# A two-layer encoder trunk on one Trainium2 core: high weight halves placed 192 bytes into wider tiles in the feature-major panels, with three small edits around it

## The chip, the core and the metric

The kernel runs on one core of one Trainium2 chip. The metric is the device time of one execution in microseconds (us); lower is better.

## The reference

The reference is two layers over an input `x` of 256 tokens by 2,048 features in float32, and a final RMSNorm. Each layer is a token mixer and a gated feed-forward network, each behind an RMSNorm and added to the residual stream:

```python
for layer in range(DEPTH):                      # DEPTH = 2
    h = _rmsnorm(x, norm_mix_g[layer])
    x = x + (_mixer_ab(...) if layer % 2 == 0 else _mixer_cd(...))
    h = _rmsnorm(x, norm_ffn_g[layer])
    x = x + _conv_ffn(h, ffn_w_up[layer], ...)  # (silu(g) * a) @ w_down, D_FF = 5632
return _rmsnorm(x, final_norm_g)
```

`_mixer_ab` projects to 7,168 columns, runs 8 heads of stick-breaking attention and 4 heads of differential attention, and projects back. `_mixer_cd` does the same with 4 heads of retention and a spatial-gating MLP. `_conv_ffn` projects to 2 x 5,632 columns, applies a causal depthwise convolution of width 3, gates, and projects back. Nearly all arithmetic is in the weight matrices, some 410 MB of float32, each read once.

## The kernel before

**Precision by splitting.** Each float32 weight block is split into a high half `hi` (a rounded copy in the type fp32r, written by ScalarE) and a low half `lo = raw - hi` (VectorE). The activations are split in the same way. TensorE then multiplies halves and adds the products up in PSUM.

**Loading.** `load_split` (L239) is the one place where weights come in. It takes a `raw` tile (128 partitions x 2,048 float32, three buffers, 1 MB), fills it by DMAs on the SyncE queue (SP) in `pieces` parts, and makes two `hi` and two `lo` tiles of 128 x 1,024 (five buffers each, L254 and L255). A tile of 1,024 float32 takes 4,096 bytes in each partition.

**Two ways to multiply.** `fm_panel` (L265) makes feature-major output for the query and key projections and for the up-projections of both feed-forward networks. One panel is 512 output features over 16 blocks of 128 input features, in four `load_split` calls. Here the weights are the stationary operand: for each of four groups of 128 output features (`m`) and four input blocks (`k`) there are two matmuls, called a pair below:

```python
nc.tensor.matmul(banks[m], hi[k][:, m * P:(m + 1) * P], xr, ...)                  # L272, 512 columns stream
nc.tensor.matmul(banks[m][:, :T], lo[k][:, m * P:(m + 1) * P], xr[:, :T], ...)    # L275, 256 columns stream
```

`xr` is an activation tile of 128 x 512 (its 256 high columns, then its 256 low ones). So `hi` meets both halves of the activation, `lo` the high half alone. Each matmul loads its own 128 x 128 stationary block before it streams. `tm_chunk` (L295) makes token-major output for all other projections. There the activation is stationary and the weights stream, in triples (L291 to L293): 512 columns each, 256 in the last quarter of `final` (L331).

**Addresses.** The pools lie one behind another in each partition: `raw`, `hi`, `lo`, the activations (`act`, 2,048 bytes a tile), then the small pools. Every `hi`, `lo` and activation tile is a multiple of 512 bytes long, and a stationary block of 128 float32 columns is 512 bytes. So before the change every block that a split matmul loads and every activation that it streams begins at the same place within 512 bytes.

**Order of the work.** Tasks (`start`, `pump`, `until`) put the small work of heads and norms between matmuls. The tile framework sets the order on each engine and the waits, from the program's order, the buffers and its own estimate of times. The first projection (`vb0`, L467) is built by hand with its activations: `First.load` sends the transposed input `x_t` on the ScalarE queue, `first_x` splits it between the weight casts, and the norm weights `gcols` (L451) scale it. 13 `warm` matmuls (L456) run on TensorE while the first data is on its way. In front of the second mixer the bias `sgu_b` comes in as a tile `sbr` (L660) and is transposed on TensorE into `sb_p` (L664).

Of the kernel before, what the change touches and what calls it, by code (L numbers as in the profile page):

```python
# [9 lines left out]
F32 = mybir.dt.float32  # L10
BF16 = mybir.dt.bfloat16
F32R = mybir.dt.float32r
# [6 lines left out]
P = 128  # L19
# [8 lines left out]
NEG = -3.0e38  # L28
ORDERED = {mybir.EngineType.DVE, mybir.EngineType.Activation}
GROUPS = (8, 12, 12, 12)  # L30


@with_exitstack
def trunk_kernel(
# [26 lines left out]
    nc = tc.nc  # L61
    cp = ctx.enter_context(tc.tile_pool(name="cp", bufs=1))
    wp = ctx.enter_context(tc.tile_pool(name="wp", bufs=3))
# [5 lines left out]
    def acc(name):  # L69
        return pp.tile([P, 512], F32, tag="acc", name=name, bufs=6)  # L70

    def small(name):
        return pp.tile([P, 512], F32, tag="small", name=name, bufs=2)
# [7 lines left out]
    def w15(name, n=384, dt=F32):  # L81
        return kp.tile([P, n], dt, tag="w15", name=name, bufs=10)
# [25 lines left out]
    def pump():  # L108
        for task in list(tasks):
            task[1] -= 1  # L110
            if task[1] <= 0:
                step(task)
# [123 lines left out]

    cnt = [0]

    def load_split(src, k, pieces=1, size=1024, before=None):  # L239
        cnt[0] += 1  # L240
        i = cnt[0]
        f = src.shape[-1]
        raw = wp.tile([P, 2048], F32, tag="raw", name=f"raw{i}")
        m = k * f
        rv = raw[:, :m].rearrange("p (k f) -> p k f", k=k)
        sv = src.rearrange("(k p) f -> p k f", p=P)
        kp_ = k // pieces
        for j in range(pieces):
            nc.sync.dma_start(rv[:, j * kp_:(j + 1) * kp_, :], sv[:, j * kp_:(j + 1) * kp_, :])
        his, los = [], []  # L250
        for j in range(0, m, 1024):
            if before is not None:
                before(j // f)
            hi = wp.tile([P, 1024], F32R, tag="hi", name=f"hi{i}_{j}", bufs=5)  # L254
            lo = wp.tile([P, 1024], F32R, tag="lo", name=f"lo{i}_{j}", bufs=5)  # L255
            for b in range(0, 1024, size):
                nc.scalar.copy(hi[:, b:b + size], raw[:, j + b:j + b + size])  # L257
                nc.vector.tensor_tensor(  # L258
                    lo[:, b:b + size], raw[:, j + b:j + b + size], hi[:, b:b + size].bitcast(F32), ALU.subtract)
            for b in range(0, 1024, f):  # L260
                his.append(hi[:, b:b + f])
                los.append(lo[:, b:b + f])
        return his, los

    def fm_panel(w, c0, xs, name):  # L265
        banks = [acc(f"fm_{name}{m}") for m in range(4)]
        for k0 in range(0, KT, 4):
            hi, lo = load_split(w[k0 * P:(k0 + 4) * P, c0:c0 + 512], 4)
            for m in range(4):
                for k in range(4):  # L270
                    xr = xs[k0 + k].rearrange("p a t -> p (a t)")
                    nc.tensor.matmul(  # L272
                        banks[m], hi[k][:, m * P:(m + 1) * P], xr,
                        start=(k0 + k == 0), stop=False, skip_group_check=True)
                    nc.tensor.matmul(  # L275
                        banks[m][:, :T], lo[k][:, m * P:(m + 1) * P], xr[:, :T],
                        start=False, stop=(k0 + k == KT - 1), skip_group_check=True)
                if m % 2 == 1:
                    pump()
        return banks  # L280
# [7 lines left out]
    def tm_mm(bank, a, t, hi, lo, st, sp):  # L288
        xh = a[:, 0, t * P:(t + 1) * P]
        xl = a[:, 1, t * P:(t + 1) * P]  # L290
        nc.tensor.matmul(bank, xh, hi, start=st, stop=False)  # L291
        nc.tensor.matmul(bank, xh, lo, start=False, stop=False)  # L292
        nc.tensor.matmul(bank, xl, hi, start=False, stop=sp)  # L293

    def tm_chunk(w, parts, n0, name, hook=None):  # L295
        banks = [acc(f"tm_{name}{t}") for t in range(2)]
        total = sum(nk for _, _, nk in parts)
        seen = 0
        for r0, xs, nk in parts:
            for k0 in range(0, nk, 4):  # L300
                kn = min(4, nk - k0)
                src = w[r0 + k0 * P:r0 + (k0 + kn) * P, n0:n0 + 512]
                if hook is None:
                    hi, lo = load_split(src, kn)
                else:
                    first = k0 == 0
                    with tc.manual_schedule(engines=ORDERED) if first else nullcontext():
                        hi, lo = load_split(
                            src, kn, 4 if first else 2, 512 if first else 1024, hook(k0))
                for k in range(kn):  # L310
                    st, sp = seen == 0, seen == total - 1
                    seen += 1
                    a = xs[k0 + k]
                    for t in range(2):
                        tm_mm(banks[t], a, t, hi[k], lo[k], st, sp)
                    if k % 2 == 1:
                        pump()
        return banks

    def residual(w, parts, norm, name):  # L320
        for n in range(4):
            banks = tm_chunk(w, parts, n * 512, f"{name}{n}")
            for t in range(2):
                xc = x_sb[:, t, n * 512:(n + 1) * 512]
                nc.vector.tensor_tensor(xc, banks[t], xc, ALU.add)
                if norm is not None:
                    norm.square(n, t)
            if norm is not None:
                start(norm.task(n), 1)
# [53 lines left out]
    def ffn(layer, norm, nxt, cols):  # L383
# [3 lines left out]
        def panel(kt0, which):  # L387
            return fm_panel(up, which * DFF + kt0 * P, norm, f"u{which}{layer}_{kt0}")
# [31 lines left out]
        early = None  # L420
        for gi, gs in enumerate(GROUPS):
            hs = []
            last = gi == len(GROUPS) - 1
            for kt0 in range(f0, f0 + gs, 4):
# [24 lines left out]
        return res  # L449

    gcols = cp.tile([P, 4, KT], F32, name="gcols")  # L451
    nc.gpsimd.dma_start(gcols, gains)
    gmix0, gffn0, gmix1, gffn1 = (gcols[:, i, :] for i in range(4))
    warm = small("warm")
    for i in range(13):
        nc.tensor.matmul(warm[:, :P], ones, ones, start=True, stop=True)  # L456
    n0 = First(gmix0, "n0")
    nc.scalar.activation(n0.rstd[:, :1], zeros, AF.Copy)
# [5 lines left out]
    def first_x(k0):  # L464
        return lambda i: n0.split(xts[k0 // 4], k0 // 4, i)

    vb0 = tm_chunk(w_in, ((0, n0, KT),), 5120, "vb0", first_x)  # L467
    def tm_copy(banks, rstd, name):
        v = m4(f"v_{name}")
# [11 lines left out]

    start(first_v(), 1)
    qb0 = fm_panel(w_in, 3072, n0, "qb0")
    until(lambda: vs)

# [41 lines left out]
    def fm_heads(c0, row, name, banks=None):  # L527
        banks = banks or fm_panel(w_in, c0, n0, name)
        dst = m4(f"qk_{name}").rearrange("p (m t) -> p m t", m=4)
        for m in range(4):  # L530
            fm_sum(banks[m], dst[:, m, :], row, f"{name}{m}")
        return dst
# [88 lines left out]
    for c in range(2):  # L621
        v = vs[0] if c == 0 else tm_copy(tm_chunk(w_in, ((0, n0, KT),), 5632, "vb1"), n0.rstd, "vb1")
        q = fm_heads(3072 + c * 512, n0.row, f"qb{c}", qb0 if c == 0 else None)
        k = fm_heads(4096 + c * 512, n0.row, f"kb{c}")
        for hh in range(2):
            start(diff_head(c * 2 + hh, q[:, hh * 2:hh * 2 + 2, :], k[:, hh * 2:hh * 2 + 2, :],
                            v, hh * 256), 2 + 2 * hh)
    for c in range(2):
        v = tm_copy(tm_chunk(w_in, ((0, n0, KT),), 2048 + c * 512, f"va{c}"), n0.rstd, f"va{c}")
        q = fm_heads(c * 512, rowq, f"qa{c}")  # L630
        k = fm_heads(1024 + c * 512, n0.row, f"ka{c}")
# [25 lines left out]
    for g in range(4):  # L657
        nc.tensor.transpose(ps[:, g * P:(g + 1) * P], sw[:, g, :], ident)
    nc.vector.tensor_copy(swt.rearrange("p g i -> p (g i)"), ps)
    sbr = cp.tile([4, P], F32, name="sbr")  # L660
    nc.sync.dma_start(sbr, sgu_b[0])
    sb = cp.tile([P, 4], F32, name="sb")
    ps = small("sb_p")
# [235 lines left out]
```

## Time and profile before

| | us |
|---|---|
| median of 3 runs | 2210.32 |
| runs | 2210.32, 2658.7, 2210.18 |
| profiled execution, own time | 2209.91 |
| its span, first to last instruction | 2208.2 |
| TensorE matmul busy (share of span) | 2195.7 (99%) |
| TensorE weight loads busy | 1868.6 (85%) |
| VectorE busy | 1414.1 (64%) |
| ScalarE busy | 1131.7 (51%) |
| GpSimd busy | 341.8 (15%) |

The profiled execution is a single one. Its own time is 1.7 us over its span and within 0.5 us of the median. A matmul's bar in the profile reaches from its first column to its modelled end, and the bars of neighbours overlap. So the pace of TensorE is read from the distance between starts, and not from the length of the bars.

### The profile page before, as it was taken

To read this page: it belongs to the slowest core of one execution; us is meant where nothing else is said; L and a number is where in the kernel's file an instruction comes from. 1 tells how busy PE (TensorE), PEld (TensorE's weight loads), DVE (VectorE), ACT (ScalarE), POOL (GpSimd) and SP (SyncE) were. 2 spreads that over 40 slices of the span, in tenths; PEclk is the share of its full clock that TensorE was granted. 3 is DMA by queue.
4 is the path that set the end of the run, shared out by engine and by line. 5 is a ranking of instruction groups with operands and counts; after the bars stand their busy time and mean duration, and the time that the engine had idled before them with its cause. 6 is when DMAs were issued, how large, how long until landed. Compare 5 with 4: busy or idle time off the path is not lost.

```text
span 2208.2 us, 29090 instructions
## 1 busy us (share of the span) xinstructions
PE 2195.7 (99%) x11297; PEld 1868.6 (85%) x11297; DVE 1414.1 (64%) x1796; ACT 1131.7 (51%) x1658; POOL 341.8 (15%) x538
## 2 busy tenths in 40 slices
PE   9999999999999999999999999999999999999998
PEld 8888888888888888888888888888888888888886
DVE  5655555586666577567756545567757757665775
ACT  6544545464554455355554455445545545544553
POOL 0110120031221022022103000002212102210320
PEclk9999999999999999999999999999999999999999
DMA  9555455556556555655655556555655655555553
GB/s 322 200 173 192 160 196 178 181 182 210 174 189 201 180 191 183 198 172 193 201 182 176 187 174 202 178 180 191 201 172 191 200 181 191 190 192 189 173 187 137
DMA packets 209903, 416.78 MB, mean 189 GB/s; under 512 B 6957, under 2 KB 10325, under 8 KB 209765
## 3 DMA queue, kind: packets, MB, share of 16 engines
q1 hardware_dynamic: 208724, 412.27, 56.8%
q10 hardware_dynamic: 1008, 2.62, 0.3%
q8 instruction: 88, 1.44, 0.3%
q14 instruction: 51, 0.41, 0.1%
q0 software_dynamic: 32, 0.03, 0.0%
HBM read 412.80 MB, written 2.89 MB: 188 GB/s over the span
## 4 chain that ended last, share of the span: by engine, by line
PE 99%; issue 0%; DVE 0%; DMA 0%; ACT 0%; POOL 0%; POOLq 0%; DVEq 0%
PE fm_u L272 30%; PE fm_u L275 15%; PE tm_d L293 7%; PE tm_d L291 7%; PE tm_d L292 7%; PE fm_ka L272 1%; PE fm_qa L272 1%; PE fm_qb L272 1%; PE fm_kb L272 1%; PE tm_oab L291 1%; PE tm_oab L293 1%; PE tm_ocd L293 1%; PE tm_oab L292 1%; PE tm_ocd L291 1%; PE tm_ocd L292 1%; PE tm_vb L292 1%
## 5 line engine op out<-in xcount | busy, mean ns | idle before, releaser
L258 DVE TENSOR_TENSOR lo<-raw,hi 128x1024 fp32r<-128x1024 f32 (+1 forms) x770 | 993.3, 1306 | 642.4 <-ACT hi L257 638.2
L257 ACT CAST hi<-raw 128x1024 fp32r<-128x1024 f32 (+1 forms) x770 | 793.7, 1047 | 735.0 <-PE fm_u L272 234.4
L272 PE MATMUL fm_u<-x_n,hi 128*128 128x512 f32 x2816 | 991.9, 397 | 0.0
L275 PE MATMUL fm_u<-x_n,lo 128*128 128x256 f32 x2816 | 789.5, 280 | 0.0
L272 PEld LDWEIGHTS fm_u<-x_n,hi 128*128 128x128 f32 x2816 | 528.7, 188 | 129.0
L275 PEld LDWEIGHTS fm_u<-x_n,lo 128*128 128x128 f32 x2816 | 531.6, 189 | 0.4
L286 POOL TENSOR_TENSOR u<-hf_u,row_n 128x256 f32<-128x256 f32 x176 | 170.8, 970 | 953.4 <-DVE hf_u L285 953.4
L291 PE MATMUL tm_d<-hi,h 128*128 128x512 f32 x688 | 268.0, 390 | 0.0
L293 PE MATMUL tm_d<-hi,h 128*128 128x512 f32 x688 | 267.8, 389 | 0.0
L292 PE MATMUL tm_d<-lo,h 128*128 128x512 f32 x688 | 267.7, 389 | 0.0
L400 ACT ACTIVATE c<-u,conv 128x256 f32<-128x256 f32 x176 | 106.0, 602 | 177.7 <-POOL u L397 174.0
L293 PEld LDWEIGHTS tm_d<-hi,h 128*128 128x128 f32 x688 | 129.1, 188 | 27.0
L291 PEld LDWEIGHTS tm_d<-hi,h 128*128 128x128 f32 x688 | 129.1, 188 | 26.7
L292 PEld LDWEIGHTS tm_d<-lo,h 128*128 128x128 f32 x688 | 129.2, 188 | 26.6
L402 DVE SCALAR_TENSOR_TENSOR c<-u,conv,c 128x256 f32<-128x256 f32 x176 | 83.9, 477 | 71.8 <-ACT c L400 71.6
L416 POOL TENSOR_TENSOR h<-c,h 128x256 fp32r<-128x256 f32 x88 | 89.6, 1018 | 145.9 <-ACT h L415 145.9
L404 DVE SCALAR_TENSOR_TENSOR c<-u,conv,c 128x256 f32<-128x256 f32 x176 | 96.9, 551 | 0.3
L285 DVE TENSOR_TENSOR hf_u<-fm_u,hf_u 128x256 f32<-128x256 f32 x176 | 73.0, 415 | 0.0
L284 ACT COPY hf_u<-fm_u 128x256 f32<-128x256 f32 x176 | 62.9, 357 | 9.9 <-PE fm_u L275 9.3
L412 ACT ACTIVATE c<-c 128x256 f32<-128x256 f32 x88 | 36.6, 415 | 44.4 <-DVE c L404 44.4
L413 DVE TENSOR_TENSOR c<-c,c 128x256 f32<-128x256 f32 x88 | 48.5, 551 | 8.1 <-ACT c L412 8.1
L125 POOL TENSOR_TENSOR rstd_n<-s_n,mhalf 128x2 f32<-128x2 f32 x4 | 2.8, 696 | 305.7 <-DVE s_n L179 305.7
(278 smaller groups left out, 2385.4 us busy)
## 6 DMA issues: line engine op xcount, KB each, us to landing
raw<-in_ffn_w_up_dram SPq DMA_DIRECT2D x176, 1024.0 KB, 5.0
raw<-in_ffn_w_down_dram SPq DMA_DIRECT2D x86, 1024.0 KB, 5.1
raw<-in_ab_w_in_dram SPq DMA_DIRECT2D x44, 1024.0 KB, 5.1
raw<-in_cd_w_in_dram SPq DMA_DIRECT2D x40, 1024.0 KB, 5.1
raw<-in_ab_w_out_dram SPq DMA_DIRECT2D x16, 1024.0 KB, 5.1
raw<-in_cd_w_out_dram SPq DMA_DIRECT2D x16, 1024.0 KB, 5.3
raw<-in_ab_w_in_dram SPq DMA_DIRECT2D x6, 512.0 KB, 9.7
x_sb<-in_x_dram SPq DMA_DIRECT2D x4, 512.0 KB, 9.4
```

The costliest lines, as they stand in the source:

```text
L257: nc.scalar.copy(hi[:, b:b + size], raw[:, j + b:j + b + size])
L258: nc.vector.tensor_tensor(lo[:, b:b + size], raw[:, j + b:j + b + size], hi[:, b:b + size].bitcast(F32), ALU.subtract)
L272: nc.tensor.matmul(banks[m], hi[k][:, m * P:(m + 1) * P], xr, start=(k0 + k == 0), stop=False, skip_group_check=True)
L275: nc.tensor.matmul(banks[m][:, :T], lo[k][:, m * P:(m + 1) * P], xr[:, :T], start=False, stop=(k0 + k == KT - 1), skip_group_check=True)
L286: nc.gpsimd.tensor_tensor(dst, half, row, ALU.mult)
L291: nc.tensor.matmul(bank, xh, hi, start=st, stop=False)
L292: nc.tensor.matmul(bank, xh, lo, start=False, stop=False)
L293: nc.tensor.matmul(bank, xl, hi, start=False, stop=sp)
L400: nc.scalar.activation(c, u[:, 2:], AF.Identity, bias=cb[:, fi:fi + 1], scale=w2[:, fi:fi + 1])
L402: nc.vector.scalar_tensor_tensor(c, u[:, 1:T + 1], w1[:, fi:fi + 1], c, ALU.mult, ALU.add)
L404: nc.vector.scalar_tensor_tensor(c, u[:, :T], w0[:, fi:fi + 1], c, ALU.mult, ALU.add)
L416: nc.gpsimd.tensor_tensor(h[:, 1, :], c, h[:, 0, :].bitcast(F32), ALU.subtract)
```

## The change

It has four parts. (1) A `hi` tile becomes 1,152 columns (4,608 bytes) wide, and the 1,024 columns in use begin at column `off` of it: 0 in general, and 48 (192 bytes) where `fm_panel` calls. (2) To make room for the five wider buffers, `sbr` moves out of the constants into the ring `w15`. The pools behind `hi` so move by 5 x 512 - 512 = 2,048 bytes in all. (3) The norm weights `gcols` are sent on the ScalarE queue instead of the GpSimd queue, and 15 instead of 13 `warm` matmuls run. (4) The second to fourth weight block of the first projection come in one DMA of 1 MB each instead of two of 512 KB.

```diff
+HI_FM = 48
-    def load_split(src, k, pieces=1, size=1024, before=None):
+    def load_split(src, k, pieces=1, size=1024, before=None, off=0):
...
-            hi = wp.tile([P, 1024], F32R, tag="hi", name=f"hi{i}_{j}", bufs=5)
+            hi = wp.tile([P, 1152], F32R, tag="hi", name=f"hi{i}_{j}", bufs=5)[:, off:off + 1024]
...
     def fm_panel(w, c0, xs, name):
...
-            hi, lo = load_split(w[k0 * P:(k0 + 4) * P, c0:c0 + 512], 4)
+            hi, lo = load_split(w[k0 * P:(k0 + 4) * P, c0:c0 + 512], 4, off=HI_FM)
...
                         hi, lo = load_split(
-                            src, kn, 4 if first else 2, 512 if first else 1024, hook(k0))
+                            src, kn, 4 if first else 1, 512 if first else 1024, hook(k0))
...
-    nc.gpsimd.dma_start(gcols, gains)
+    nc.scalar.dma_start(gcols, gains)
...
-    for i in range(13):
+    for i in range(15):
         nc.tensor.matmul(warm[:, :P], ones, ones, start=True, stop=True)
...
-    sbr = cp.tile([4, P], F32, name="sbr")
+    sbr = w15("sbr", P)[:4, :]
```

The matmuls of the panels stand in the same order as before; what moves in the order are the small parts. The first place is the head of the ScalarE queue, with the norm weights `gcols` and the transposed input `xt`. Before:

```order
L206 DMA xt_105<-in_x_t_dram 128x512
L458 ACT_TABLE_LOAD
L458 ACTIVATE rstd_n_103<-zeros 128x1
L206 DMA xt_105<-in_x_t_dram 128x512
L206 DMA xt_108<-in_x_t_dram 128x1024
L206 DMA xt_110<-in_x_t_dram 128x1024
L206 DMA xt_112<-in_x_t_dram 128x1024
L132 ACTIVATE x_n_123<-xt_105,gcols 128x256
```

And after it, with every line number one higher:

```order
L453 DMA gcols<-in_gains_dram 128x64
L459 ACT_TABLE_LOAD
L459 ACTIVATE rstd_n_105<-zeros 128x1
L207 DMA xt_107<-in_x_t_dram 128x512 x2
L207 DMA xt_110<-in_x_t_dram 128x1024
L207 DMA xt_112<-in_x_t_dram 128x1024
L207 DMA xt_114<-in_x_t_dram 128x1024
L133 ACTIVATE x_n_125<-xt_107,gcols 128x256
```

`gcols` now stands first, and the first part of `xt` stands behind it and behind the load of the activation table.

The second place is TensorE at the start of the second mixer, where the last down-projection ends and `tm_zv`, the first chunk of the new input projection, begins. `swt_p` and `sb_p` are the transposes of the spatial weights and of `sbr`, `xt_n` that of the residual stream. Before:

```order
L658 MATMUL swt_p<-ident,sw 128x128 x4
L664 MATMUL sb_p<-ident,sbr 128x4
L291 MATMUL tm_zv_10036<-hi_0_10040,x_n_9646 128x512
...
L293 MATMUL tm_zv_10037<-hi_0_10040,x_n_9649 128x512
L160 MATMUL xt_n_10060<-ident,x_sb 128x128 x4
L160 MATMUL xt_n_10065<-ident,x_sb 128x128 x4
```

And after it:

```order
L293 MATMUL tm_zv_10035<-lo_1024_10044,x_n_9654 128x512
L294 MATMUL tm_zv_10035<-hi_1024_10043,x_n_9654 128x512
L665 MATMUL sb_p<-ident,sbr 128x4
L161 MATMUL xt_n_10059<-ident,x_sb 128x128 x4
L161 MATMUL xt_n_10064<-ident,x_sb 128x128 x4
L292 MATMUL tm_zv_10036<-hi_1024_10043,x_n_9654 128x512
```

`sb_p` moves from ahead of the chunk to behind 21 of its matmuls, and the eight `xt_n` transposes from behind 12 to behind 21.

The third place is the SyncE queue, where the DMA of `sbr` (2 KB) stood among loads of the first layer:

```order
L645 DMA rp<-in_rope_dram 128x2x256
L661 DMA sbr<-in_sgu_b_dram 4x128
L249 DMA raw_626<-in_ab_w_in_dram 128x4x512
```

Now it stands behind the fifth weight load of the second mixer:

```order
L250 DMA raw_10164<-in_cd_w_in_dram 128x4x512
L250 DMA raw_10202<-in_cd_w_in_dram 128x4x512
L662 DMA sbr<-in_sgu_b_dram 4x128
L250 DMA raw_10236<-in_cd_w_in_dram 128x4x512
```

The DMA of `sbr` moves from the first layer to a few microseconds ahead of its use.

## Rows read from the trace of the kernel before

**Rows 1.** The page: span, busy time by engine, granted clock in 40 slices.

```profile
span 2208.2 us, 29090 instructions
...
PE 2195.7 (99%) x11297; PEld 1868.6 (85%) x11297; DVE 1414.1 (64%) x1796; ACT 1131.7 (51%) x1658; POOL 341.8 (15%) x538
...
PEclk9999999999999999999999999999999999999999
```

**Rows 2.** The page's costliest groups (busy us, mean ns | idle before, releaser).

```profile
L258 DVE TENSOR_TENSOR lo<-raw,hi 128x1024 fp32r<-128x1024 f32 (+1 forms) x770 | 993.3, 1306 | 642.4 <-ACT hi L257 638.2
L257 ACT CAST hi<-raw 128x1024 fp32r<-128x1024 f32 (+1 forms) x770 | 793.7, 1047 | 735.0 <-PE fm_u L272 234.4
L272 PE MATMUL fm_u<-x_n,hi 128*128 128x512 f32 x2816 | 991.9, 397 | 0.0
L275 PE MATMUL fm_u<-x_n,lo 128*128 128x256 f32 x2816 | 789.5, 280 | 0.0
```

**Rows 3.** TensorE in 100 us stretches of panels: window, us, busy, matmuls, clock, DMA.

```profile
410.00:510.00 100.00, 100.00 (x578) 1.00 0.57 189
554.00:654.00 100.00, 100.00 (x569) 1.00 0.56 185
...
1476.00:1576.00 100.00, 100.00 (x576) 1.00 0.58 190
```

**Rows 4.** Timeline of TensorE, first stretch of rows 3 (start us, length us).

```profile
449.76 0.40 PE L272 MATMUL fm_u<-x_n,hi 128*128 128x512 f32 x1
...
451.15 0.40 PE L272 MATMUL fm_u<-x_n,hi 128*128 128x512 f32 x1
```

**Rows 5.** Timeline of TensorE, second stretch of rows 3.

```profile
599.92 0.40 PE L272 MATMUL fm_u<-x_n,hi 128*128 128x512 f32 x1
...
600.98 0.40 PE L272 MATMUL fm_u<-x_n,hi 128*128 128x512 f32 x1
```

**Rows 6.** Timeline of TensorE in `final`, where triples of 512 columns become 256.

```profile
2195.16 0.39 PE L293 MATMUL fin<-hi,h 128*128 128x512 f32 x1
...
2196.52 0.39 PE L293 MATMUL fin<-hi,h 128*128 128x512 f32 x1
...
2196.86 0.28 PE L292 MATMUL fin<-lo,h 128*128 128x256 f32 x1
...
2197.34 0.28 PE L293 MATMUL fin<-hi,h 128*128 128x256 f32 x1
```

**Rows 7.** Matmuls of L272 for `fm_u` alone by window.

```profile
396.00:514.00 118.00, 111.38 (x320) 60.00 (x320) 1.00 0.56 183
...
1460.00:1580.00 120.00, 111.49 (x320) 59.86 (x320) 1.00 0.56 184
```

**Rows 8.** Timeline of the first 8 us (idle before and its releaser in brackets).

```profile
1.13 5.22 PE L456 MATMUL warm<-ones 128*128 128x128 f32 x26 [1.13 <-DVE zeros L98]
...
1.38 0.73 POOL L452 DMA_DIRECT2D gcols<-in_gains_dram  x1 [0.33 <-issue]
...
6.43 0.91 ACT L132 ACTIVATE x_n<-xt,gcols 128x256 fp32r<-128x256 f32 x2 [3.67 <-DMA gcols<-in_gains_dram]
...
7.90 0.51 PE L291 MATMUL tm_vb<-hi,x_n 128*128 128x512 f32 x1 [1.55 <-ACT hi L257]
```

**Rows 9.** Busy time (PE, PEld, DVE, ACT, POOL), clock, DMA share, GB/s.

```profile
10.00:20.00 10.00, 10.00 (x41) 8.19 (x40) 8.33 (x14) 8.23 (x15) 0.00 (x0) 0.89 1.05 390
```

**Rows 10.** Waits in the first 32 us (in total, times, longest).

```profile
ACT hi L257 <- DMA raw<-in_ab_w_in_dram: 6.2, 3, 3.2
```

**Rows 11.** DMA issues in the first 35 us (KB each, median us to landing).

```profile
raw<-in_ab_w_in_dram SPq DMA_DIRECT2D x4, 256.0 KB, 4.6
...
rb<-in_rel_bias_dram SPq DMA_DIRECT2D x1, 0.5 KB, 4.7
```

**Rows 12.** Timeline at the start of the second mixer.

```profile
1135.52 6.67 SPq L249 DMA_DIRECT2D raw<-in_cd_w_in_dram  x2
...
1136.18 0.22 PE L664 MATMUL sb_p<-ident,sbr 4*128 4x4 f32 x1
...
1139.23 1.03 PE L160 MATMUL xt_n<-ident,x_sb 128*128 128x128 f32 x8
```

## The prediction

> **What bounds the kernel now.** I read the page's first part first. TensorE is busy for 2195.7 us of a span of 2208.2 us, and its granted clock is 9 in all 40 slices, so at the upper of its two levels (2.4 GHz) but for moments [rows 1]. TensorE sets the time, and only two things can move the total much: the number of matmuls, or the distance between their starts. The number stays (but for two warm-up matmuls), so the question is the distance.
>
> Next I read the groups. The split matmuls of the up-projections (L272 and L275) take most of TensorE's time and never sat idle before a start [rows 2]. ScalarE's casts to `hi` and VectorE's subtractions to `lo` wait for TensorE and for each other, and are together far under the span [rows 2]. They are ahead of TensorE and not behind it.
>
> The distance itself comes from windows and from single starts. In two windows of 100 us, both full of the same matmuls, TensorE makes 578 and 576; in a third, also without a gap, 569 [rows 3]. The same work so runs at two paces. Single starts give them exactly: in the first window four pairs take 451.15 - 449.76 = 1.39 us, or 347 ns a pair [rows 4]; in the third, three pairs take 600.98 - 599.92 = 1.06 us, or 353.3 ns [rows 5]. The windows agree: 2 x 100 us / 578 = 346 ns and 2 x 100 us / 569 = 351.5 ns, each a little low since a window also counts matmuls that only reach into it.
>
> The last chunk gives the pieces of a pair. There triples of 512 columns follow each other at (2196.52 - 2195.16) / 6 = 226.7 ns, and those of 256 columns at (2197.34 - 2196.86) / 4 = 120 ns [rows 6]. So 256 further columns cost 106.7 ns, 512 cost 213.3 ns, and 13.3 ns are left per matmul whatever its length. Each of these matmuls loads its own stationary block. A pair of 512 and 256 columns should so take 226.7 + 120 = 346.7 ns. That is the fast pace; the slow one is 6.7 ns more. Over one long stretch all sixteen blocks of a panel, which lie in different tiles and at different multiples of 512 bytes, keep one pace, so a multiple of 512 bytes does not matter. What an offset of 192 bytes does, no row of before shows: all operands there begin at the same place within 512 bytes.
>
> **How many pairs run at each pace.** Panels hold 3,328 pairs: 2,816 of `fm_u` [rows 2] and 4 x 128 of the query and key panels. The two fast stretches, 396 to 514 us and 1460 to 1580 us, hold 320 each [rows 7]. I count 640 fast and 2,688 slow; a few pairs of the first panels are fast too, and a few at the head of each fast stretch are slow, which is under half a microsecond. The mean is (640 x 346.7 + 2,688 x 353.3) / 3,328 = 352.0 ns.
>
> **Part 1, the offset.** It acts on the loads of `hi` in the panels alone. Such a load runs while the `lo` matmul before it streams its 256 columns, the short window of the pair. The loads of `lo` and all of `tm_chunk` keep their alignment. From below (the most it can give): the `hi` load's own 13.3 ns and the 6.7 ns of the slow pace both go. Then each pair takes 333.3 ns, and the gain is 2,688 x 20 + 640 x 13.3 = 62.3 us. From above: the load gets dearer by one more step of 6.7 ns and the fast pace is gone, so each pair takes 360 ns, and 2,688 x 6.7 + 640 x 13.3 = 26.5 us are lost. In the middle lies the pace that the kernel already shows, 346.7 ns for every pair: 2,688 x 6.6 = 17.8 us gained. I take this one. The two paces at one and the same alignment say that the extra 6.7 ns is a matter of how the `hi` load falls in with the stream beside it, and an offset shifts just that, while the 13.3 ns stand in every matmul of the trace, in windows both short and long.
>
> Here a page of the Trainium skill speaks against the change. TensorE: Matmul & The Clock Gate, section "Step-by-step: what each phase is for", says that loading the next weights takes no read bandwidth from the running matmul, since the two have read ports of their own. By that rule the offset gives nothing, and the sum stays at the time of before. The trace does not quite fit it: two paces of the same instructions [rows 4, 5] show that something between load and stream depends on more than their lengths. No row says that it is the address.
>
> ScalarE writes `hi` and VectorE reads it at the new place. I cost that at nothing: 770 casts of 1047 ns and 770 subtractions of 1306 ns are hidden behind TensorE, with 735 and 642 us of idle time before them [rows 2]. If it made each 10% longer, the idle time would still cover it.
>
> **Part 2, `sbr` in the ring.** Its DMA now stands behind the fifth load of the second mixer, and so may first be sent at about 1135.52 + 0.37 (that load's issue) = 1135.9 us [rows 12]. A 512-byte load took 4.7 us to land [rows 11], so it lands near 1140.6 us. On TensorE `sb_p` now stands behind 21 matmuls instead of ahead of them: 1136.18 + 21 x 0.227 = 1140.9 us [rows 6, 12]. It comes just in time. Bounds: no wait, or 1.5 us if it lands as late as the whole 1 MB load ahead of it lets it; what is queued behind it on TensorE is the whole program. I take 0.3 us lost. The next weight load on SyncE is sent 0.6 us later, and three buffers of lead hide that. That `xt_n` comes nine matmuls later costs nothing, since its result is used in later blocks.
>
> **Parts 3 and 4, the start.** ScalarE waits 3.67 us for `gcols`, until 6.43 us, and the first real matmul starts at 7.90 us [rows 8]. On the ScalarE queue `gcols` is sent first. The quarter of weights that the first cast needs lands at about 0.82 + 4.6 = 5.4 us [rows 11], so the chain can start 1.0 us earlier. Two more warm-up matmuls are four more passes of 5.22 / 26 = 0.20 us [rows 8], which end about when the data comes. TensorE then has no gap there, and the stretch at half clock (1.2 GHz) behind the gap, which shows as 0.89 in the window from 10 to 20 us [rows 9], may go: 0.11 x 10 us = 1.1 us. The most is thus 2.1 us gained. But the DMA engines are full in that window (share 1.05, 390 GB/s [rows 9]), and ScalarE waited 6.2 us for weights there already [rows 10]: a TensorE that starts earlier waits for the next block. That block now comes in one piece of 1 MB, whose first half is only seen when the second has landed, 512 KB / 390 GB/s = 1.3 us later. So the worst is 1.3 us lost. I take 0.7 us gained.
>
> **Sum.** From the profiled execution's own 2209.9 us (1.7 us over its span, and 0.4 us under the median of 2210.3): 2209.9 - 17.8 + 0.3 - 0.7 = 2191.7. I say 2192.
>
> **The rivals.**
>
> *The address doesn't matter (the change does not do what it says).* Load and stream do not meet in memory, and which pace a stretch takes depends on how it was entered. For it: the fast stretches begin at 396 and 1460 us, each time behind a norm, at the same addresses as the slow ones. Against it: nothing in the trace, which has no second alignment. Time: 2209.9 + 0.3 - 0.7 = 2209.5 us. The mix of fast and slow stretches may fall out otherwise, which gives 2205 to 2214 us. The skill's rule above leads to this one. Chance 0.27.
>
> *The `hi` load gets wholly out of the stream's way.* For it: 13.3 ns over the columns in every split matmul look like a price of each load, and the offset may pay it for half the loads. Against it: the price is the same in long and short windows, as a fixed cost of the instruction would be. All of it gives 2209.9 - 62.3 - 0.4 = 2147 us; between this and the forecast lies a pair of 340 ns, with 2171 us. Chance for 333 to 341 ns: 0.27.
>
> *The offset makes it worse.* The `hi` load now meets the stream in the middle of the short window, where before it met it at the head, and no pair can settle into the fast pace. Price: 360 ns a pair, 2209.9 + 26.5 - 0.4 = 2236 us. It ends over the time of before from the point where the mean pair is over 352.0 ns. For it: the short window is the one with no slack, 120 ns for 256 columns [rows 6]. Against it: the loads there already carry one step of 6.7 ns, and a second was seen nowhere. Chance 0.10.
>
> **How the numbers follow.** The forecast, 346.7 ns a pair with the start and `sbr` between their bounds, has 0.36; its own range is 2186 to 2198 us. The range over all reaches down nearly to the whole of the second rival, 2148 us, and up over the first, 2213 us; it leaves out the third and the edges. Of the second rival somewhat over half is under 2165.7 us, 2% below the median of before. 2% is about what a measurement of this kernel can tell from no change. With a little for a gain outside these cases, faster by over 2% gets 0.19. Slower by over 2% (2254.5 us) needs a pair of some 366 ns, more than the third rival's price, and gets 0.03. The rest, 0.78, is within 2%.
>
> **What would show it.** Right: windows of 100 us in the middle of the panels hold 576 to 578 matmuls everywhere, L272 starts 347 ns apart, and the triples of `tm_chunk` stay at 226.7 ns. Starts of 353 ns in the long stretches would mean that the offset does nothing, 333 to 340 ns that the load's own price went, 354 ns or more that it got dearer. At the start, the wait for `gcols` should be gone, the first real matmul should come at about 6.9 us, and waits for `raw` should take its place. At the second mixer, a wait of TensorE for the DMA of `sbr` of over a microsecond would make that term wrong.

## The result, and the profile after

The changed kernel takes 2171.6 us (median of 4 runs, 2171.22 to 2172.84) against 2210.3 us before: a ratio of 0.9826, 95% interval 0.9807 to 0.9845. One run of the kernel before was slow, 2658.7 us, and is left out of the ratio. The gain of 38.7 us is inside the forecast range and over twice the forecast of 18.

The page's head and its costliest groups, in the form of [rows 1] and [rows 2]; every line number is one higher than before:

```profile
span 2169.4 us, 29090 instructions
...
PE 2155.6 (99%) x11301; PEld 1851.1 (85%) x11301; DVE 1428.6 (66%) x1796; ACT 1126.2 (52%) x1658; POOL 341.1 (16%) x537
...
PEclk9999999999999999999999999999999999999999
...
L259 DVE TENSOR_TENSOR lo<-raw,hi 128x1024 fp32r<-128x1024 f32 (+1 forms) x770 | 1009.4, 1328 | 589.0 <-ACT hi L258 584.8
L258 ACT CAST hi<-raw 128x1024 fp32r<-128x1024 f32 (+1 forms) x770 | 791.4, 1046 | 674.9 <-PE tm_d L294 205.2
L273 PE MATMUL fm_u<-x_n,hi 128*128 128x512 f32 x2816 | 958.8, 389 | 0.0
L276 PE MATMUL fm_u<-x_n,lo 128*128 128x256 f32 x2816 | 777.3, 276 | 0.0
```

TensorE is still busy for 99% of the span, at the upper of its two clock levels, and the panels still never wait. The same work has become denser. TensorE in 100 us stretches of panels, to be held against [rows 3] (window, us, busy, matmuls, clock, DMA share, GB/s):

```profile
405.00:505.00 100.00, 100.00 (x585) 1.00 0.57 190
550.00:650.00 100.00, 100.00 (x590) 1.00 0.57 190
...
1450.00:1550.00 100.00, 100.00 (x591) 1.00 0.58 192
```

Before, the counts there were 578, 569 and 576. The starts give the pace (timeline of TensorE: start us, length us):

```profile
599.44 0.39 PE L273 MATMUL fm_u<-x_n,hi 128*128 128x512 f32 x1
599.66 0.28 PE L276 MATMUL fm_u<-x_n,lo 128*128 128x256 f32 x1
...
601.82 0.39 PE L273 MATMUL fm_u<-x_n,hi 128*128 128x512 f32 x1
```

Seven pairs take 601.82 - 599.44 = 2.38 us, or 340.0 ns a pair; at this place a pair took 353.3 ns [rows 5]. It is the pace of nearly the whole run: of the groups of three pairs that follow each other without a break, 3,201 of 3,262 take exactly 1,020 ns between starts. Neither of the old paces, 1,040 and 1,060 ns for three pairs, is left as a stretch.

Summed over the trace (from the start of each matmul to the next start), the panels fell from 1172.8 to 1133.6 us, the triples of `tm_chunk` and `final` from 967.4 to 965.4 us, and the rest rose from 58.2 to 61.0 us. Distances of over 450 ns between triples, which are waits, are counted to the rest here; with them the triples take 969.7 and 969.9 us. The panels' 39.2 us are the gain; the span fell by 38.8. The triples keep the 226.7 ns of [rows 6]; nine matmuls of them take 2.04 us:

```profile
899.78 0.39 PE L292 MATMUL tm_d<-hi,h 128*128 128x512 f32 x1
...
901.82 0.39 PE L292 MATMUL tm_d<-hi,h 128*128 128x512 f32 x1
```

The start went the other way. Its timeline after, against [rows 8]:

```profile
0.80 0.42 ACTq L453 DMA_DIRECT2D gcols<-in_gains_dram  x1
1.12 5.49 PE L457 MATMUL warm<-ones 128*128 128x128 f32 x30 [1.12 <-DVE zeros L99]
1.31 0.87 ACTq L207 DMA_DIRECT2D xt<-in_x_t_dram  x2
3.82 3.31 ACTq L207 DMA_DIRECT2D xt<-in_x_t_dram  x3
7.18 0.91 ACT L133 ACTIVATE x_n<-xt,gcols 128x256 fp32r<-128x256 f32 x2 [4.44 <-DMA raw<-in_ab_w_in_dram]
8.65 0.50 PE L292 MATMUL tm_vb<-hi,x_n 128*128 128x512 f32 x1 [2.04 <-ACT hi L258]
```

The wait for `gcols` is gone, but the first activation is split at 7.18 instead of 6.43 us and the first real matmul starts at 8.65 instead of 7.90 us. The releaser in brackets is inferred. The rows of ScalarE's queue say more: the three last issues of `xt` stretch from 3.82 to 7.13 us, and `x_n` starts 0.05 us behind them. Of the two parts of `xt` of 256 KB the trace has one landing only: here that of the second part, 5.7 us after its issue, at 7.44 us; before, that of the first part, 3.9 us after its issue. So these two cannot be compared. DMA issues in the first 10 us:

```profile
xt<-in_x_t_dram ACTq DMA_DIRECT2D x2, 256.0 KB, 5.7
```

The clock in the window from 10 to 20 us is now 1.00 instead of 0.89 [rows 9], but TensorE is busy there for only 8.72 of 10 us (busy PE, PEld, DVE, ACT, POOL, clock, DMA share, GB/s):

```profile
10.00:20.00 10.00, 8.72 (x38) 6.64 (x37) 7.41 (x13) 7.56 (x14) 0.00 (x0) 1.00 1.04 396
```

The rest of that window is spent in waits for the second weight block, which now lands in one piece of 1 MB, at 14.29 us; before, its first half landed at 12.53 us. By the start of the first panel (`fm_qb`) the change has lost 1.0 us in these two executions. After:

```profile
14.31 1.05 ACT L258 CAST hi<-raw 128x1024 fp32r<-128x1024 f32 x1 [1.07 <-DMA raw<-in_ab_w_in_dram]
15.41 0.50 PE L292 MATMUL tm_vb<-hi,x_n 128*128 128x512 f32 x1 [0.53 <-ACT hi L258]
16.67 0.50 PE L293 MATMUL tm_vb<-lo,x_n 128*128 128x512 f32 x1 [0.76 <-DVE lo L259]
...
32.90 0.40 PE L273 MATMUL fm_qb<-x_n,hi 128*128 128x512 f32 x1
```

And before:

```profile
31.87 0.39 PE L272 MATMUL fm_qb<-x_n,hi 128*128 128x512 f32 x1
```

### The profile page after: what moved, and what is told of

It reads as the page before. It is cut to its first block, busy times and chain, and to the rows that moved or that the text cites. A ratio compares the mean times of both kernels' runs of the same rounds, so it can differ in the third digit from the quotient of the medians.

```text
span 2169.4 us, 29090 instructions
## 1 busy us (share of the span) xinstructions
PE 2155.6 (99%) x11301; PEld 1851.1 (85%) x11301; DVE 1428.6 (66%) x1796; ACT 1126.2 (52%) x1658; POOL 341.1 (16%) x537
## 3 DMA queue, kind: packets, MB, share of 16 engines
q10 hardware_dynamic: 1152, 2.65, 0.3%
## 4 chain that ended last, share of the span: by engine, by line
PE 98%; DMA 1%; DVE 0%; issue 0%; ACT 0%; SPq 0%; POOLq 0%; POOL 0%; DVEq 0%
PE fm_u L273 29%; PE fm_u L276 15%; PE tm_d L294 7%; PE tm_d L293 7%; PE tm_d L292 7%; PE tm_oab L292 1%; PE fm_kb L273 1%; PE tm_oab L294 1%; PE tm_oab L293 1%; PE tm_ocd L292 1%; PE tm_ocd L294 1%; PE tm_ocd L293 1%; PE fm_qa L273 1%; PE fm_qb L273 1%; PE fm_ka L273 1%; PE tm_va L292 1%
## 5 line engine op out<-in xcount | busy, mean ns | idle before, releaser
L259 DVE TENSOR_TENSOR lo<-raw,hi 128x1024 fp32r<-128x1024 f32 (+1 forms) x770 | 1009.4, 1328 | 589.0 <-ACT hi L258 584.8
L258 ACT CAST hi<-raw 128x1024 fp32r<-128x1024 f32 (+1 forms) x770 | 791.4, 1046 | 674.9 <-PE tm_d L294 205.2
L273 PE MATMUL fm_u<-x_n,hi 128*128 128x512 f32 x2816 | 958.8, 389 | 0.0
L276 PE MATMUL fm_u<-x_n,lo 128*128 128x256 f32 x2816 | 777.3, 276 | 0.0
L417 POOL TENSOR_TENSOR h<-c,h 128x256 fp32r<-128x256 f32 x88 | 89.8, 1020 | 145.7 <-ACT h L416 145.7
```

The source lines that it names most:

```text
L259: nc.vector.tensor_tensor(lo[:, b:b + size], raw[:, j + b:j + b + size], hi[:, b:b + size].bitcast(F32), ALU.subtract)
L417: nc.gpsimd.tensor_tensor(h[:, 1, :], c, h[:, 0, :].bitcast(F32), ALU.subtract)
```

## The experiments

Theory A: the pace of a pair is set by where the loaded block stands against the streamed tile within some hundred bytes. Theory B: the offset itself does nothing; wider tiles or the new start moved the stream into a better rhythm, which it then keeps, as before had two paces at one alignment. Below, "mean pair" is the mean distance from one `hi` matmul's start to the next over all pairs of a run without a long break (under 450 ns; 352.1 ns before, 340.3 ns after, where a few short breaks lift it over 340.0). Only the four first runs, and the two on the start, were timed in several rounds; the others are one run each, beside the kernel before at 2209.75 to 2210.56 us. A mean pair stands for some 3,300 pairs even in a single run.

### One part at a time

Offset 0 and 512 bytes, all else as in the changed kernel:

```diff
-HI_FM = 48
+HI_FM = 0      # e1_offset_0;  128 in e2_offset_512
```

> The changed kernel with the offset set to 0; the hi tiles stay 1,152 columns wide, so every buffer sits where it sits in the changed kernel. Theory A (the place of the loaded hi block against the streamed x tile, within 512 bytes, decides how long the load takes beside the short lo matmul): the panel pairs return to 346.7 or 353.3 ns, a time of 2192 to 2211 us (1.0 to 1.3 us of it the new start). Theory B (the place does not matter; the wider tiles, or the new order at the start, moved the stream into a better rhythm that it then keeps): the pairs stay at 340.0 ns and the time at 2171 to 2173 us.

> The changed kernel with the offset at 128 columns, 512 bytes, which fills the wider tile. Theory A with a period of 512 bytes: as offset 0, pairs of 346.7 or 353.3 ns and 2192 to 2211 us. Theory A with a longer period, or a rule that any offset will do: pairs of 340.0 ns and 2171 to 2173 us. Theory B: 340.0 ns, 2171 to 2173 us.

The changed kernel with the start of before (offset alone), and the kernel before with the new start alone:

```diff
 # e3_offset_only, from the changed kernel
-    nc.scalar.dma_start(gcols, gains)
+    nc.gpsimd.dma_start(gcols, gains)
-    for i in range(15):
+    for i in range(13):
-        src, kn, 4 if first else 1, 512 if first else 1024, hook(k0))
+        src, kn, 4 if first else 2, 512 if first else 1024, hook(k0))
 # e4_start_only: the three lines the other way, in the kernel before
```

> The kernel before with the wider tiles, the 192-byte offset and the moved bias row, but with its own start (norm weights on GpSimd's queue, 13 warm matmuls, first weight load in two pieces). Theory A: pairs of 340.0 ns, and 0.8 to 1.5 us less than the changed kernel, since its first real matmul began at 7.9 instead of 8.65 us: 2170.0 to 2170.9 us. Theory B, if the start sets the rhythm: pairs of 346.7 or 353.3 ns, 2192 to 2210 us.

> The kernel before with the edits of the start alone (norm weights on ScalarE's queue, 15 warm matmuls, first weight load in one piece); no offset, tiles of 1,024 columns. Theory A: the pairs keep 346.7 and 353.3 ns, and the time is 2210.5 to 2212 us, 0.5 to 1.5 us over the kernel before. Theory B, if the start sets the rhythm: pairs of 340.0 or 346.7 ns through the whole run, 2171 to 2193 us.

| | time, us | ratio to before (95%) | mean pair, ns |
|---|---|---|---|
| e1_offset_0 | 2210.57 | 1.0001 (0.9992 to 1.0011) | 352.1 |
| e2_offset_512 | 2211.13 | 1.0004 (0.9995 to 1.0014) | 352.1 |
| e3_offset_only | 2171.03 | 0.9821 (0.9804 to 0.9837) | 340.4 |
| e4_start_only | 2210.79 | 1.0002 (0.9993 to 1.0012) | 352.1 |

TensorE in the run with offset 0, at the place shown above for the changed kernel:

```profile
599.17 0.40 PE L273 MATMUL fm_u<-x_n,hi 128*128 128x512 f32 x1
...
601.29 0.40 PE L273 MATMUL fm_u<-x_n,hi 128*128 128x512 f32 x1
```

Six pairs in 2.12 us are 353.3 ns, the slow pace of [rows 5]. The wide tiles are there and the new start too; only the 192 bytes are missing, and with them the whole gain. Theory B falls. An offset of 512 bytes is as good as none. The new start alone gives no gain and no loss that can be measured. e3_offset_only lies just over its expected 2170.0 to 2170.9 us.

### Which distance counts

192 unused bytes between the weight tiles and the activations move x and leave `hi` in its place; in the other run `lo` is moved instead of `hi`:

```diff
 # e5_x_moved (with HI_FM = 0)
+    xp = ctx.enter_context(tc.tile_pool(name="xp", bufs=1))
     ap_ = ctx.enter_context(tc.tile_pool(name="ap", bufs=28))
...
+    pad = xp.tile([P, 48], F32, name="pad")
+    nc.gpsimd.memset(pad, 0.0)
 # e6_lo_moved
-            hi = wp.tile([P, 1152], F32R, tag="hi", name=f"hi{i}_{j}", bufs=5)[:, off:off + 1024]
-            lo = wp.tile([P, 1024], F32R, tag="lo", name=f"lo{i}_{j}", bufs=5)
+            hi = wp.tile([P, 1024], F32R, tag="hi", name=f"hi{i}_{j}", bufs=5)
+            lo = wp.tile([P, 1152], F32R, tag="lo", name=f"lo{i}_{j}", bufs=5)[:, off:off + 1024]
```

> Offset 0, and 192 unused bytes put between the weight tiles and the tiles of x, so that x moves by 192 bytes and the hi blocks stay where they were. If it is the distance between the loaded block and the streamed tile that counts: pairs of 340.0 ns, 2170.5 to 2172.5 us, as with the hi blocks moved. If it is the place of the hi block alone (its address within 512 bytes): pairs of 346.7 and 353.3 ns, 2210 to 2212 us, as offset 0 gave.

> The hi tiles back at 1,024 columns with no offset, and the lo tiles 1,152 wide with their halves 192 bytes in. The lo block is loaded under the 512-column matmul, the hi block under the 256-column one. If the short matmul's window is what the load overruns: lo's place is of no use, pairs stay at 346.7 and 353.3 ns, 2208 to 2212 us. If both loads disturb the stream in the same way: half of the gain, about 346 ns and 2190 us. If any load that is out of line is enough: 340.0 ns, 2171 us.

And two other offsets, `HI_FM = 16` and `HI_FM = 64`:

> The changed kernel with an offset of 64 bytes in place of 192. If only near alignment within 512 bytes does harm, and 64 bytes are enough to be clear of it: 340.0 ns and 2171 to 2173 us. If the loaded block and the streamed columns must be further apart: 346.7 or 353.3 ns and 2192 to 2211 us, or worse than offset 0.

> The changed kernel with an offset of 256 bytes, half the period that offset 512 pointed to. Clear of alignment: 340.0 ns and 2171 to 2173 us. If the harm has a period of 256 bytes: 346.7 or 353.3 ns and 2192 to 2211 us.

e5_x_moved took 2224.8 us, e6_lo_moved 2203.8, e7_offset_64 2179.0 and e8_offset_256 2212.4. In the first, `hi` stands apart from x as in the changed kernel but for the sign, and yet the mean pair is 353.4 ns: the distance of `hi` to x alone does not decide. Its time is above both expectations, since a moved x also shifts the triples, which I had not thought of: there x is the block that is loaded, and three matmuls took 687 instead of 680 ns. So from here on I compare the pairs, and the times only second. e6_lo_moved gained a little, 350.1 ns. Offset 256 has the mean pair of offset 0, 352.1 ns.

Two readings were left: `hi`'s own address counts (it did not move in e5), or both distances count, of `hi` and of `lo` to x. The four remaining combinations of moving the three tell these apart, with pads of 192 bytes ahead of the weight tiles (a pool `yp` ahead of `wp`) and ahead of x:

```diff
+    yp = ctx.enter_context(tc.tile_pool(name="yp", bufs=1))
     wp = ctx.enter_context(tc.tile_pool(name="wp", bufs=3))
...
+    pad0 = yp.tile([P, 48], F32, name="pad0")
+    nc.gpsimd.memset(pad0, 0.0)
 # e9_all_moved: pad0, HI_FM = 0          e10_hi_x_moved: pad of e5, HI_FM = 48
 # e11_lo_x_moved: pad0, HI_FM = 16       e12_hi_lo_moved: pad0, pad of 16 columns, HI_FM = 0
```

> Offset 0 and 192 unused bytes ahead of the weight tiles: hi, lo and x all move by 192 bytes and stand to each other as in the kernel before. If only distances between them count: pairs as before, 346.7 and 353.3 ns, 2208 to 2212 us. If the address of the loaded hi block counts by itself: 340.0 ns, 2171 us.

> The changed kernel (hi 192 bytes in) with x moved by 192 bytes as well, so that lo alone stays: hi again in line with x, lo 192 bytes behind. If the address of the hi block counts by itself: 340.0 ns, 2171 to 2173 us. If distances count: like the run with lo moved, which has the mirror image of these distances, about 350 ns and 2200 to 2206 us.

> 192 unused bytes ahead of the weight tiles and an offset of 64 bytes, so that the hi blocks stand, within 256 bytes, at the address of the kernel before while lo and x have moved by 192 bytes. The distances are those of the offset of 64 bytes. If distances count: 340.0 ns in most of the run, 2176 to 2182 us as there. If the address of the hi block counts by itself: 350 ns or more, 2200 to 2226 us.

> Pads of 192 bytes ahead of the weight tiles and of 64 bytes ahead of x, offset 0: hi and lo stand 192 bytes on, x (within 256 bytes) where it was. If the address of the hi block counts by itself: 340.0 ns, 2171 to 2173 us. If distances count, this has the mirror image of those of the run with x moved: 353 ns, 2215 to 2226 us; in line with each other, hi and lo give no gain.

All combinations, with the distances taken within 256 bytes (what was moved; x's distance to the streamed weights counts in the triples):

| moved | hi - x | lo - x | mean pair, ns | x - weights in triples | three matmuls of a triple, ns | time, us |
|---|---|---|---|---|---|---|
| nothing (e1) | 0 | 0 | 352.1 | 0 | 680 | 2210.6 |
| all (e9) | 0 | 0 | 352.1 | 0 | 680 | 2212.2 |
| hi (after) | 192 | 0 | 340.3 | 0 | 680 | 2171.6 |
| hi by 64 (e7) | 64 | 0 | 342.1 | 0 | 680 | 2179.0 |
| lo and x (e11) | 64 | 0 | 343.3 | 0 | 680 | 2183.3 |
| lo (e6) | 0 | 192 | 350.1 | 0 | 680 | 2203.8 |
| hi and x (e10) | 0 | 64 | 346.9 | 192 | 686 to 700 | 2209.5 |
| x (e5) | 64 | 64 | 353.4 | 192 | 687 | 2224.8 |
| hi and lo (e12) | 192 | 192 | 352.5 | 64 | 697 to 703 | 2239.1 |

The address of `hi` by itself does not count: it is the same in the rows "hi", "hi and x", "hi and lo" and "all", with 340.3, 346.9, 352.5 and 352.1 ns. With all three moved alike, the pace is that of none moved. What decides is how the three stand to each other: `hi` apart and `lo` in line with x is the good case, both moved alike is no better than both in line. The third distance, of `hi` to `lo`, is fixed by the other two, so the table can also be read by it: in the four rows where it is 0, the pair takes 352 to 353 ns wherever x stands. It does not decide alone either, since `hi` stands 192 bytes from `lo` (within 256) in the rows "hi" and "hi and x", with 340.3 and 346.9 ns. The runs do not show which two of the three meet. The triples were fastest with all in line; a distance of 64 or 192 slowed them.

The expectations for e10 and e12 took mirrored distances to be equal. That held for the pairs of e12 and not for e10, which has 346.9 ns against 350.1 in e6; both times missed, because of the triples. In e12 three of their matmuls take 697 to 703 ns. Timeline of TensorE in e12_hi_lo_moved (L298 to L300 are the triple), in `tm_d` and in the last chunk of `final`, where triples of 512 columns become 256:

```profile
899.92 0.39 PE L300 MATMUL tm_d<-hi,h 128*128 128x512 f32 x1
...
902.02 0.40 PE L300 MATMUL tm_d<-hi,h 128*128 128x512 f32 x1
...
2226.41 0.28 PE L298 MATMUL fin<-hi,h 128*128 128x256 f32 x1
...
2226.98 0.28 PE L300 MATMUL fin<-hi,h 128*128 128x256 f32 x1
```

Nine matmuls of 512 columns take 2.10 us (233 ns each), against 2.04 in the changed kernel. But five of 256 columns take 0.57 us, 114 ns each, where the last four of the same matmuls in line took 120 ns each [rows 6]. So the 120 ns were no fixed length of a short matmul: they go when the loaded block stands elsewhere.

### The period

> The changed kernel with an offset of 128 bytes, half of the period of 256 bytes that the runs so far show. If the loss goes with how near the hi block stands to the streamed tile and the lo block within that period, the middle is as good as 192 bytes: 340.0 ns and 2171 to 2173 us. If the harm has a period of 128 bytes: pairs of 346.7 and 353.3 ns and 2209 to 2213 us.

> The changed kernel with an offset of 32 bytes. 64 bytes gave 340 ns in most of the run and 350 ns in the rest. If the gain grows with the distance: between offset 0 and 64, a mean pair of 343 to 351 ns and 2182 to 2209 us. If any distance will do: as 64 bytes, 2177 to 2183 us. If 64-byte pieces are what counts: as offset 0, 2209 to 2213 us.

> The changed kernel with an offset of 448 bytes, 192 + 256. If the pace of the panels has a period of 256 bytes: as 192 bytes, 340.0 ns throughout and 2171 to 2173 us. If 64 and 192 differ only in their distance from the block's start: a mean pair of 342 ns or more and 2177 us or more.

> The changed kernel with an offset of 320 bytes, 64 + 256. With a period of 256 bytes: as 64 bytes, 340.0 ns in most of the run and about 350 ns in the rest, 2177 to 2183 us. If 192 bytes or more are simply enough: 340.0 ns throughout and 2171 to 2173 us. With a period of 128 bytes: as 64 and 192 bytes, between 2171 and 2183 us, with no way to tell which.

The offset in the changed kernel, nothing else altered (`HI_FM` = bytes / 4):

| offset, bytes | 0 | 32 | 64 | 128 | 192 | 256 | 320 | 448 | 512 |
|---|---|---|---|---|---|---|---|---|---|
| mean pair, ns | 352.1 | 351.2 | 342.1 | 352.1 | 340.3 | 352.1 | 342.1 | 340.3 | 352.1 |
| time, us | 2210.6 | 2207.9 | 2179.0 | 2212.6 | 2171.6 | 2212.4 | 2178.1 | 2171.2 | 2211.1 |

448 does as 192, 320 as 64, 256 and 512 as 0: the period is 256 bytes. The gain does not grow with the distance, since 128 gives none. At 128 the old mean hides another rhythm: five pairs in 600.98 - 599.22 = 1.76 us, 352 ns, from a cycle of five pairs that offset 0 does not show (timeline of e15_offset_128):

```profile
599.22 0.39 PE L273 MATMUL fm_u<-x_n,hi 128*128 128x512 f32 x1
...
600.98 0.39 PE L273 MATMUL fm_u<-x_n,hi 128*128 128x512 f32 x1
```

64 differs from 192 in that some stretches stay slow. TensorE in stretches of panels in e7_offset_64:

```profile
405.00:505.00 100.00, 100.00 (x572) 1.00 0.52 180
...
1450.00:1550.00 100.00, 100.00 (x592) 1.00 0.54 184
```

The first is the place where offset 0 has its fast pace; here it is the slow one. So 64 bytes leave two paces, as offset 0 does, and 192 bytes only one.

### The start

The offset with the start of before, and one edit of the new start added each time:

```diff
 # e13_norms_on_act
-    nc.gpsimd.dma_start(gcols, gains)
+    nc.scalar.dma_start(gcols, gains)
 # e14_one_piece
-        src, kn, 4 if first else 2, 512 if first else 1024, hook(k0))
+        src, kn, 4 if first else 1, 512 if first else 1024, hook(k0))
```

> The kernel with the offset and the start of before, and one edit of the new start added: the norm weights on ScalarE's queue. If their 256-byte packets ahead of x on that queue hold up x: first real matmul at 8.6 to 10.5 us, as in the runs with the whole new start, and a time 0.5 to 1.5 us over the offset alone, 2171.5 to 2172.5 us. If the 1 MB load holds x up: first real matmul at 7.0 to 7.9 us, 2170 to 2171 us.

> The kernel with the offset and the start of before, and the other edit added: the second weight load in one piece of 1 MB. If the 1 MB load is what delays the start: first real matmul at 8.6 us or later and 2171.5 to 2172.5 us. If the norm weights' packets are: first real matmul at 7.9 us and 2170.5 to 2171.5 us.

e13_norms_on_act: 2170.53 us, ratio 0.9822 (0.9808 to 0.9837). e14_one_piece: 2171.45 us, 0.9829 (0.9812 to 0.9845). The first real matmul of e13 and of e14, in this order:

```profile
8.14 0.79 PE L292 MATMUL tm_vb<-hi,x_n 128*128 128x512 f32 x1 [2.18 <-ACT hi L258]
```

```profile
8.12 0.50 PE L292 MATMUL tm_vb<-hi,x_n 128*128 128x512 f32 x1 [1.35 <-ACT hi L258]
```

Either edit alone costs 0.2 us there, in one profiled execution each, so both expectations that blamed one edit missed. With both (and two more warm matmuls) it starts at 8.22 to 10.90 us in 16 runs, with the old start at 7.90 and 7.89. So the first matmul is late with both edits, and by an amount that changes from run to run; with one edit alone a single execution each cannot show that spread.

The first panel tells more than the first matmul. It starts at 31.16 us in e3_offset_only, 31.77 in e13 and 33.06 in e14: at 31.16 to 31.87 us in the three runs that load in halves, at 32.70 to 35.17 in all 17 that load in pieces of 1 MB. So the pieces are what costs time there. In the time of the whole kernel the ratios' intervals overlap: 2170.53 us in e13, 2171.03 in e3, 2171.45 in e14 and 2171.6 in the changed kernel. The four runs of e13 and of e14 point the same way as the first panel, 2169.90 to 2171.07 against 2171.37 to 2173.07 us. No version beats the changed kernel by more than that.

## Why the prediction was right in direction and half in size

**The bound and the count of paces** were right. Only the distance between TensorE's starts moved, and the mean pair of before, 352.0 ns in the prediction, is 352.1 ns over the whole trace.

**Part 1 is the step that failed**, and in it the sentence "In the middle lies the pace that the kernel already shows, 346.7 ns for every pair". It gave 17.8 us; the term measured 39.2 us. The mechanism was right in the main: the place of the loaded `hi` block makes the extra time, the offset shifts that, and without it the gain is gone (e1, e3). But it is not the `hi` load alone that counts (e6, e12), and the short window is not where most was lost: from 560 to 640 us the next start comes 236.1 ns behind a `hi` matmul and 117.2 ns behind a `lo` matmul before, 226.9 and 113.1 ns after. The ground for the size was wrong: "13.3 ns are left per matmul whatever its length", read as a fixed cost from 226.7 and 120 ns [rows 6]. Two lengths gave a straight line, but the shorter one was itself slowed by its load: 256 columns take 113.3 ns in the pairs after the change (340.0 - 226.7) and 114 ns in the last chunk of e12. 113.3 is half of 226.7, so nothing is left over per matmul, and a pair with its loads out of the way is 226.7 + 113.3 = 340.0 ns. That leaves nothing for the lower bound of 333.3 ns; no run shows a shorter pace than 340.0.

The row to doubt was at hand: with no fixed cost, the 512-column triples give 0.443 ns a column, and 256 columns at 120 ns are then 6.7 ns late, just the step by which the two paces differ. The rows even held a clean pair: from 2196.52 to 2196.86 us one matmul of 512 and one of 256 columns go by in 0.34 us [rows 6]. The forecast took the fast pace for the clean one; it was itself 6.7 ns over it. That 226.7 + 120 met the fast pace was chance: its parts, from 420 to 500 us before, are 231.8 and 114.8 ns.

**The rivals.** That the load gets wholly out of the way came true for 340 ns a pair; its full price, 333.3 ns, did not. That the time named there for 340 ns, 2171 us, is the measured one is luck: by the prediction's own terms it is 2209.9 - 40.0 - 0.4 = 2169.5 us, and the start took 1.0 us where 0.7 were to be gained. Two smaller slips change nothing: 2,688 x 6.6 ns are 17.7 us, and 2% below the median of before is 2166.1 us. That the address doesn't matter fell with e1, e2 and e3. That an offset makes it worse did not happen here, but is real elsewhere: e12 took 2239 us, through the triples.

The Trainium skill, TensorE: Matmul & The Clock Gate, section "Step-by-step: what each phase is for", has the next load take no read bandwidth from the running matmul. In effect the runs do not agree: the same instructions take 340.0 or 353.3 ns a pair by addresses alone. Whether it is read bandwidth that is lost, they do not show.

**What stayed put** stayed: multiples of 512 bytes do nothing (e2), the triples keep 226.7 ns, and the casts and subtractions at the new place take 1046 and 1328 ns, with 675 and 589 us of idle time left.

**Part 2** was right in size, and its wait is not shown. SyncE sends `sbr` at 1114.37 us, and TensorE's load for it starts at 1119.36 us, 5.0 us later (timeline of after; the idle time in brackets is the weight load's):

```profile
1114.37 0.36 SPq L662 DMA_DIRECT2D sbr<-in_sgu_b_dram  x1
...
1119.04 0.39 PE L294 MATMUL tm_zv<-hi,x_n 128*128 128x512 f32 x1
...
1119.36 0.14 PEld L665 LDWEIGHTS sb_p<-ident,sbr 4*128 4x128 f32 x1 [0.35 <-issue]
```

0.32 us from the matmul ahead, where 0.23 is the pace, leave some 0.1 us lost against the forecast 0.3. The trace has no landing of `sbr`, and it does not put the idle time down to the DMA. So whether the data came just in time, as forecast, or well ahead stays open.

**Parts 3 and 4** were wrong in sign: 0.7 us gained was forecast, with the first real matmul at about 6.9 us; it came at 8.65 us, and the first panel 1.0 us later than before. The wait for `gcols` went, but x itself was close behind: the step that failed is "so the chain can start 1.0 us earlier", which looked at the weights' landing alone. The second part of `xt` landed at 7.44 us, against 6.22 in e3_offset_only, which has the start of before, and `x_n` stood behind the last issue of `xt` until 7.13 us. The gap ahead of the first real matmul did not close; it grew from 1.55 to 2.04 us. The clock in the window behind it is 1.00 all the same, but so it is in e3_offset_only, so that term was not the change's to gain. What came true is the worst case named there: the second half of a 1 MB piece holds up the first, and every run with these pieces starts its first panel later. How norm weights and pieces add up on the queues is not shown.

**Left open:** why the distances act as they do, with a period of 256 bytes, good at 64 and 192 and poor at 32 and 128, and why triples are fastest with all in line. The runs show it as an effect of addresses; they do not show where in the chip load and stream meet.

## What to carry to other kernels

Where each matmul brings its own stationary block, look at the distance between starts for two lengths of stream, and compute the time per column from the fastest stretch of the longest: a short matmul that is late by that measure may be held up by a load, and moving the loaded block by 64 or 192 bytes against the streamed one is a cheap trial. Do not read a fixed cost from two points of which one may be slowed. Try the offset for each loop by itself: an offset between loaded block and stream cured the pairs here and slowed the triples, and moving both loaded blocks of the pair gave nothing.

## What the runs showed of the hardware

- Beside loads that do not disturb it, the stream takes 0.443 ns a column at a granted clock of 1.00, for 512 columns (226.7 ns) as for 256 (113.3 ns), with a load of 128 columns in each.
- The places of loaded blocks and streamed tile to each other, within 256 bytes, move a pair between 340 and 353 ns and a triple between 680 and 703 ns. Moving all operands together changes nothing (352.1 ns in e9_all_moved and e1_offset_0).
- ScalarE stood at its own DMA issues: with `gcols` ahead on its queue, the last issue of `xt` was over at 7.13 us and `x_n` came 0.05 us behind it. In e15_offset_128 these were 9.39 and 9.44 us, in e13_norms_on_act 6.63 and 6.68 us; it is 0.04 to 0.05 us in all 17 runs with `gcols` on that queue. Whether `x_n` would come sooner with these issues elsewhere was not tried.
